# Weight parts in one buffer and one transfer, weight transfers issued by GpSimd, and 22 instead of 28 transfers in each pair's inverse, in a hybrid GLA and RWKV-7 layer

## The chip, the cores and the metric

The kernel runs on one core of a Trainium2 chip. The metric is the device time of one execution in microseconds (us), as the median of several runs. The core has five engines with an instruction queue each: TensorE (PE in the profile, with its weight loads as PEld), VectorE (DVE), ScalarE (ACT), GpSimd (POOL) and SyncE (SP), which computes nothing and here only issues transfers (DMA). Each queue works strictly in order: an instruction that waits for a semaphore holds up everything behind it on its engine. Sixteen DMA engines move the data between the core's memory (SBUF) and the chip's main memory (DRAM).

## The reference

One decoder layer on 1024 prompt tokens and 8 sample tokens. All of it in float32:

```python
p = einsum('btd,dn->btn', x, w_in)                 # 1024 -> 9360 columns
p_gla, p_rwkv, p_gate = split(p)
# GLA, 4 heads:  S_t = diag(a_t) S_{t-1} + k_t^T v_t ;  o_t = q_t S_t
# RWKV-7, 16 heads of 64:
#   S_t = S_{t-1} (diag(w_t) - kk_t^T (kk_t a_t)) + v_t^T k_t ;  y_t = S_t r_t
m = sigmoid(gate_a) * (o_gla @ w_up_gla) + sigmoid(gate_b) * (o_rwkv @ w_up_rwkv)
y = layernorm(alpha * x + m @ w_out)
```

The outputs are y for both groups of tokens, the new states of both branches and the last projected RWKV row.

## The kernel before, in words

**Matmuls in three parts.** TensorE's fast number format keeps fewer bits than float32, so every weight and every activation is split into a high part and a rest (low part), and each product is the sum of three matmuls: high by high, high by low, low by high. In the profile the weights' parts are `whi` and `wlo`, those of the activations `xh` and `xl`, and the three kinds of rows are `proj<-xh,whi`, `proj<-xl,whi`, `proj<-xh,wlo`.

**Two passes over the tokens.** The prompt is cut into two halves of 512 tokens; the first half carries the 8 sample tokens too. For each half the kernel goes through 73 blocks of 128 columns of `w_in`. After both, it multiplies with `w_up_gla` and `w_up_rwkv` (eight blocks each, for each half) and at last with `w_out`.

**The weights' way (`load_w`).** A block needs two pieces of 512 rows by 128 columns. In the first pass, a piece is loaded raw (`wraw<-w_in`, 256 KB, three buffers), cast to `whi` on ScalarE, subtracted to `wlo` on VectorE or GpSimd, and both parts are kept in DRAM (`wh<-whi`, `wl<-wlo`, 256 KB each). In the second pass the two parts are loaded back (`whi<-wh`, `wlo<-wl`) with no work for ScalarE and VectorE. `whi` and `wlo` have four buffers each. The 64 pieces of `w_up_gla` and `w_up_rwkv` are loaded raw and split each time.

**The RWKV pairs.** Heads are worked on in eight pairs for each half of the tokens, 16 in all, in chunks of 64 tokens. For each pair `front` makes a triangular matrix for each chunk and head (`GG`, tile `gg`), whose inverse is needed. The inverse goes by 32 by 32 blocks: the diagonal blocks are gathered through DRAM (`LD<-gg`, 4 transfers; `wide<-LD`, 4; the block below the diagonal `Lp<-gg`, 4), 31 steps of two VectorE instructions each invert all of them at once (`Xt<-X,wide` and `X<-X,Xt`), and the result goes back through DRAM (`XD<-X`, 4; `XT<-XD`, 4; `Xs<-XD`, 8). That is 28 transfers a pair. `back` and `turn` finish the inverse, `chain` runs the recurrence over the chunks on TensorE (`pch`), and `norm` writes `o_rwkv`.

**What sets the order.** The kernel is written as Python generators, one for each stream of work. A planner (class `Order`) asks each stream for its next operation, prices it (`price`, `transfer`), and writes down the operation that can start first by its own clock of each engine, with priorities (`PRIO`, `ON_PE`) between streams. The result is one fixed list of instructions for each engine. Where an operation may run on VectorE or on GpSimd (`self.E`), the planner takes the engine that it expects to end first. All transfers are issued by SP (`self.S`), in the planner's order. The transfers of one queue use eight semaphores in turn, so a transfer waits on its queue until the one eight places ahead of it has landed.

All instructions that the planner writes stand at one line of the code (L219 in the profile, the call inside a helper), so the groups in the profile are told apart by their tiles, not by their lines.

Of the kernel before, what the change touches and what calls it, by code (L numbers as in the profile page):

```python
# [20 lines left out]
P = 128  # L21
# [11 lines left out]
C = 64  # L33
# [20 lines left out]
WBUF = {"whi": ([P, 512], 4), "wlo": ([P, 512], 4), "wraw": ([P, 512], 3)}  # L54
# [8 lines left out]


# [82 lines left out]
def price(eng, name, out, args, ins):  # L147
# [60 lines left out]
class Engine:  # L208
# [3 lines left out]
    def __getattr__(self, name):  # L212
        def make(out, *args, **kw):
# [8 lines left out]
            if eng == "S":  # L222
# [18 lines left out]
class Order:  # L241
# [4 lines left out]
    def __init__(self, nc):  # L246
        self.P, self.A, self.V, self.G, self.S, self.E, self.C = (Engine(**e) for e in (
            {"P": nc.tensor}, {"A": nc.scalar}, {"V": nc.vector}, {"G": nc.gpsimd}, {"S": nc.sync},
# [82 lines left out]
    def start(self, op):  # L331

        best = None
        for eng, fn, cost in op.ways:
            free, t = self.time[eng] + (SWITCH if eng == "P" and op.tiles != self.tiles else 0.0), 0.0
            for x in (op.out, *op.ins):
                at, by = self.ready.get(x.tensor.name, (0.0, None))
                if eng == "S" and by == "D" and x is op.out:
                    continue
# [28 lines left out]
    def run(self):  # L368
        while self.streams:
# [24 lines left out]
            self.time[op.eng] = max(self.time[op.eng], t + cost)  # L394
# [8 lines left out]
            if op.eng == "S":  # L403
# [3 lines left out]
            self.ready[op.out.tensor.name] = end, "D" if op.eng == "S" else op.eng  # L407
# [5 lines left out]
class Kern(Order):  # L413
# [217 lines left out]
    def load_w(self):  # L631
# [5 lines left out]
        def keep(src, c0, j, hi, lo):  # L637
            for v, x in zip("hl", (hi, lo)):
                t = self.dr.tile([P, 512], F32, name=f"w{v}{c0}_{j}")
                kept.setdefault((c0, j), []).append(t)  # L640
                yield self.S.dma_start(t, x.bitcast(F32))

        def high():
            n = 0
            while True:
                yield lambda: len(raws) > n
                hi = yield from self.get("whi")
                yield self.A.copy(hi, raws[n][0])
                his.append(hi)
# [4 lines left out]
        def low():  # L654
            for n in range(count):
                yield lambda: len(his) > n
                lo = yield from self.get("wlo")
                raw, src, c0, j, i = raws[n]
                yield self.E.tensor_sub(lo, raw, his[n].bitcast(F32))
                self.free(raw)  # L660
                if src is self.a["w_in"] and i == 0:
                    yield from keep(src, c0, j, his[n], lo)
                self.ws.append((his[n], lo))
                los.append(lo)
# [18 lines left out]
    def blocks(self):  # L683
        xs = None
        for b in self.plan:
# [13 lines left out]
            while todo:  # L699
# [7 lines left out]
                for k in range(NK):  # L707
# [4 lines left out]
                    hi, lo = (x[:, k % 4 * P:k % 4 * P + P] for x in w[k // 4])  # L712
# [8 lines left out]
                    if fin and k % 4 == 3:  # L721
                        self.free(*w[k // 4])
# [378 lines left out]
    def front(self, c, p, st, d):  # L1101
# [4 lines left out]
        AZ, GG = (x.rearrange("p (c k h t) -> p c k h t", c=NCH, k=2, h=2) for x in (az, gg))  # L1106
# [83 lines left out]
        for q in range(4):  # L1190
            yield self.S.dma_start(L_[NU * q:NU * q + NU], LD.rearrange("n c s t -> (n c) (s t)"))
        Lp = (yield from self.get("Lp")).rearrange("p (y t) -> p y t", t=P)
        for n, b in enumerate(QS):
            h = n % 2
            yield self.S.dma_start(Lp[b, :, b], GG[QS[0], n // 2::2, 0, h, 32:64])
# [13 lines left out]
        for q in range(2):  # L1209
            b = slice(32 * q, 32 * q + 32)  # L1210
            for h in range(2):
                n = 2 * q + h
                yield self.S.dma_start(XT[HS[h]][b, :, h, b], XD[n * NCH:(n + 1) * NCH].rearrange("c s t -> s c t"))
        Xs = yield from self.get("Xs")
        xp = Xs[:, :2 * P].rearrange("p (q y t) -> p q y t", q=2, t=32)
        for n, b in enumerate(QS):
            for q in range(2):
# [579 lines left out]
```

## Time and profile before

| | us |
|---|---|
| median of 3 runs (lowest, highest) | 1544.31 (1543.3, 1545.22) |
| the profiled execution's own time | 1537.94 |
| span in the profile | 1536.1 |
| PE busy | 1492.0 |
| DVE busy | 1146.4 |
| ACT busy | 866.7 |
| POOL busy | 87.3 |
| moved by DMA | 330.68 MB in 377056 packets |

In the profile's views, "x146" counts instructions, and the idle time of an engine is put down to the instruction or transfer whose end released it. An entry such as `SPq` is time on SP's queue, which issues transfers. The first pass runs to about 600 us, the second to about 1211 us, the products with `w_up_gla` and `w_up_rwkv` to about 1430 us, and `w_out` fills the rest.

### The profile page before, as it was taken

To read this page: it belongs to the slowest core of one execution; us is meant where nothing else is said; L and a number is where in the kernel's file an instruction comes from. 1 tells how busy PE (TensorE), PEld (TensorE's weight loads), DVE (VectorE), ACT (ScalarE), POOL (GpSimd) and SP (SyncE) were. 2 spreads that over 40 slices of the span, in tenths; PEclk is the share of its full clock that TensorE was granted. 3 is DMA by queue.
4 is the path that set the end of the run, shared out by engine and by line. 5 is a ranking of instruction groups with operands and counts; after the bars stand their busy time and mean duration, and the time that the engine had idled before them with its cause. 6 is when DMAs were issued, how large, how long until landed. Compare 5 with 4: busy or idle time off the path is not lost. (4 is left out here: it accounts for less than half of the span.)

```text
span 1536.1 us, 32633 instructions
## 1 busy us (share of the span) xinstructions
PE 1492.0 (97%) x11352; PEld 1304.9 (85%) x11352; DVE 1146.4 (75%) x3044; ACT 866.7 (56%) x2218; POOL 87.3 (6%) x202
## 2 busy tenths in 40 slices
PE   9999989999999999999999999999999999999998
PEld 8999979899999998788777778878777898988786
DVE  5785879788968896777776888888875774665665
ACT  5665576667666676564654565456346745654210
POOL 0010000001000000000001020100100000000000
PEclk9999999999999999999999999999999999999999
DMA  9878968798869887865677557656664779798522
GB/s 302 268 224 245 323 191 256 200 294 255 256 172 291 251 264 201 254 179 147 170 210 197 166 151 215 203 156 185 181 206 117 239 212 270 243 289 276 182 87 83
DMA packets 377056, 330.68 MB, mean 215 GB/s; under 512 B 131219, under 2 KB 262428, under 8 KB 376892
## 3 DMA queue, kind: packets, MB, share of 16 engines
q1 hardware_dynamic: 376892, 328.60, 70.7%
q8 instruction: 90, 1.47, 0.4%
q14 instruction: 74, 0.61, 0.1%
HBM read 198.35 MB, written 118.61 MB: 206 GB/s over the span
## 5 line engine op out<-in xcount | busy, mean ns | idle before, releaser
L219 PE MATMUL proj<-xh,whi 128*128 128x264 f32 (+2 forms) x1880 | 618.3, 329 | 5.9 <-ACT whi L219 2.7
L219 PE MATMUL proj<-xh,wlo 128*128 128x264 f32 (+2 forms) x1880 | 617.7, 329 | 0.3 <-DVE wlo L219 0.2
L219 PE MATMUL proj<-xl,whi 128*128 128x264 f32 (+2 forms) x1880 | 617.7, 329 | 0.0
L219 PEld LDWEIGHTS proj<-xh,whi 128*128 128x128 f32 x1880 | 355.6, 189 | 32.6 <-ACT row L219 3.1
L219 PEld LDWEIGHTS proj<-xh,wlo 128*128 128x128 f32 x1880 | 356.0, 189 | 24.2 <-DVE wlo L219 1.0
L219 PEld LDWEIGHTS proj<-xl,whi 128*128 128x128 f32 x1880 | 356.0, 189 | 23.4 <-issue 1.4
L219 DVE TENSOR_TENSOR wlo<-wraw,whi 128x512 fp32r<-128x512 f32 x207 | 142.2, 690 | 73.6 <-ACT whi L219 65.0
L219 ACT CAST whi<-wraw 128x512 fp32r<-128x512 f32 x210 | 129.9, 620 | 98.6 <-PE proj L219 23.1
L219 DVE TENSOR_TENSOR row<-row 128x256 f32<-128x256 f32 (+8 forms) x330 | 165.2, 509 | 20.1 <-DMA row<-state_rwkv 6.7
L219 ACT ACTIVATE row<-row 128x512 f32<-128x512 f32 (+3 forms) x229 | 138.1, 610 | 19.2 <-DVE row L219 11.2
L219 DVE TENSOR_TENSOR Xt<-X,wide 128x60 f32<-128x60 f32 (+24 forms) x496 | 105.8, 213 | 26.4 <-DMA wide<-LD 14.1
L219 DVE TENSOR_TENSOR X<-X,Xt 128x60 f32<-128x60 f32 (+24 forms) x496 | 104.7, 211 | 12.2
L219 ACT COPY rh<-pch 128x128 f32<-128x128 f32 x116 | 30.9, 267 | 131.1 <-PE pch L219 130.6
L219 ACT ACTIVATE row<-proj,omu 128x256 f32<-128x256 f32 (+1 forms) x99 | 54.1, 548 | 69.6 <-PE proj L219 68.4
L219 PE MATMUL big<-row 128*128 128x128 f32 (+4 forms) x466 | 87.0, 323 | 5.9 <-DVE row L219 4.2
L219 ACT ACTIVATE s0p<-wide,pc 64x64 f32<-64x64 f32 x256 | 89.0, 347 | 1.9
L219 POOL TENSOR_TENSOR row<-row 128x256 f32<-128x256 f32 (+7 forms) x55 | 49.5, 904 | 573.4 <-DVE row L219 313.2
L219 DVE SCALAR_TENSOR_TENSOR wide<-pch,pc,s0p 64x64 f32<-64x64 f32 x224 | 63.0, 281 | 22.8 <-PE pch L219 18.8
L219 DVE SCALAR_TENSOR_TENSOR row<-proj,pv,row 128x255 f32<-128x255 f32 (+1 forms) x99 | 56.3, 569 | 24.7 <-ACT tail L219 14.8
L219 PEld LDWEIGHTS big<-row 128*128 128x128 f32 (+3 forms) x466 | 59.0, 179 | 17.5 <-ACT row L219 6.2
L219 ACT COPY row<-big 128x128 f32<-128x128 f32 (+5 forms) x146 | 42.8, 316 | 44.9 <-PE big L219 43.9
L392 ACT ACT_TABLE_LOAD x52 | 66.7, 1283 | 0.9
(282 smaller groups left out, 2472.9 us busy)
## 6 DMA issues: line engine op xcount, KB each, us to landing
wraw<-w_in SPq DMA_DIRECT2D x146, 256.0 KB
wh<-whi SPq DMA_DIRECT2D x146, 256.0 KB
wl<-wlo SPq DMA_DIRECT2D x146, 256.0 KB
whi<-wh SPq DMA_DIRECT2D x146, 256.0 KB
wlo<-wl SPq DMA_DIRECT2D x146, 256.0 KB
wide<-LD SPq DMA_DIRECT2D x64, 128.0 KB
wraw<-w_up_gla SPq DMA_DIRECT2D x32, 256.0 KB
wraw<-w_up_rwkv SPq DMA_DIRECT2D x32, 256.0 KB
```

What stands on the lines that cost most here:

```text
L219: ways.append((eng, lambda call=call: call(out, *args, **kw), price(eng, name, out, args, ins)))
L392: self.nc.scalar.preload_act_table_set(self.table)
```

## The change

Three things change, and the planner then writes a new order on all engines.

1. **One buffer for both parts.** `whi` and `wlo` become one tile `wb` of 1024 columns, high part in the first 512, low part in the last 512; four buffers as before, and the same bytes of SBUF. Keeping a piece in DRAM is one transfer of 512 KB where it was two of 256 KB, and so is loading it back.
2. **GpSimd issues the weights' transfers.** A new name `self.Q` stands for GpSimd as an issuer of transfers, with a price of 1.0 us in the planner (SP's is 0.48). All raw loads after the ninth, all 146 transfers that keep a piece and all 146 that load one back go there: 137 + 64 + 146 + 146 = 493. The first nine raw loads stay on SP. GpSimd has its own eight semaphores for transfers.
3. **22 transfers in an inverse.** The tile `GG` is laid out with the two halves of each chunk's columns outermost, so that `LD<-gg` takes 2 transfers where it took 4, and `Xs<-XD` 4 where it took 8. The bytes and the runs of 32 numbers stay as they were.

```diff
-WBUF = {"whi": ([P, 512], 4), "wlo": ([P, 512], 4), "wraw": ([P, 512], 3)}
+WBUF = {"wb": ([P, 1024], 4), "wraw": ([P, 512], 3)}
...
+SAME = {"Q": "G"}
...
+    if eng == "Q":
+        return 1.0
...
+            e = SAME.get(op.eng, op.eng)
+            self.time[e] = max(self.time[e], t + cost)
...
-        def keep(src, c0, j, hi, lo):
-            for v, x in zip("hl", (hi, lo)):
-                t = self.dr.tile([P, 512], F32, name=f"w{v}{c0}_{j}")
-                kept.setdefault((c0, j), []).append(t)
-                yield self.S.dma_start(t, x.bitcast(F32))
+        def keep(src, c0, j, x):
+            kept[c0, j] = self.dr.tile([P, 1024], F32, name=f"w{c0}_{j}")
+            yield self.Q.dma_start(kept[c0, j], x.bitcast(F32))
...
-                hi, lo = (yield from self.get("whi")), (yield from self.get("wlo"))
-                for x, t in zip((hi, lo), kept[c0, j]):
-                    yield self.S.dma_start(x.bitcast(F32), t)
-                self.ws.append((hi, lo))
+                x = yield from self.get("wb")
+                yield self.Q.dma_start(x.bitcast(F32), kept[c0, j])
+                self.ws.append(x)
...
-            op = self.S.dma_start(raw.rearrange("p (k c) -> p k c", c=P),
+            op = (self.Q if n > 8 else self.S).dma_start(raw.rearrange("p (k c) -> p k c", c=P),
...
-        LD = self.dr.tile([4, NCH, 32, 32], F32, name=f"LD{c.i}{p}")
+        LD = self.dr.tile([2, 2 * NCH, 32, 32], F32, name=f"LD{c.i}{p}")
         for q in range(2):
             b = slice(32 * q, 32 * q + 32)
-            for h in range(2):
-                yield self.S.dma_start(LD[2 * q + h].rearrange("c s t -> s c t"), GG[b, :, 0, h, b])
+            yield self.S.dma_start(LD[q].rearrange("u s t -> s u t"), GU[b, :, b])
...
         for n, b in enumerate(QS):
-            for q in range(2):
-                u = (2 * q + n % 2) * NCH + n // 2
-                yield self.S.dma_start(xp[b, q], XD[u:(2 * q + n % 2 + 1) * NCH:2].rearrange("c s t -> s c t"))
+            yield self.S.dma_start(xp[b], XD.rearrange("(m n) s t -> n s m t", n=4)[n])
```

Two places show what happens to the order. The first is the weight stream early in the first pass. Before, it stands on SP (`wh_…<-whi` and `wl_…<-wlo` keep the two parts of a piece, the numbers name the DRAM tile):

```order
L219 DMA wh_0_516<-whi 128x512
L219 DMA wraw<-w_in 128x4x128
L219 DMA wl_0_519<-wlo 128x512
L219 DMA row<-lora 64x512 x3
L219 DMA wh_1_567<-whi 128x512
L219 DMA wraw<-w_in 128x4x128
L219 DMA wl_1_574<-wlo 128x512
```

After the change, the same stream stands on GpSimd (POOL), one transfer to keep a piece for each raw load:

```order
L223 DMA wraw<-w_in 128x4x128
L223 DMA w_0_498<-wb 128x1024
L223 DMA wraw<-w_in 128x4x128
L223 DMA w_1_542<-wb 128x1024
L223 DMA wraw<-w_in 128x4x128
L223 DMA w_0_574<-wb 128x1024
```

Three SP entries for a piece have become two POOL entries, and nothing of the weights is left on SP between the other transfers.

The second place is the last pair's inverse, near the end of the RWKV work, with the loads of `o_rwkv` (`row<-o_rwkv`) for the next products right behind it. On SP before:

```order
L219 DMA XD_17660<-X 256x1x32 x4
L219 DMA row<-w_out 128x512 x2
L219 DMA wraw<-w_up_gla 128x4x128
L219 DMA mg_127<-row 128x520
L219 DMA XT_170<-XD_17660 32x8x32 x4
L219 DMA Xs<-XD_17660 32x4x32 x8
L219 DMA row<-o_rwkv 128x520
L219 DMA mg_128<-row 128x520
L219 DMA row<-o_rwkv 128x520 x7
L219 DMA az_168<-az_168 64x8x64
L219 DMA wraw<-w_up_gla 128x4x128
```

On SP after the change:

```order
L223 DMA XD_16836<-X 256x1x32 x4
L223 DMA row<-sg_97 128x520
L223 DMA row<-w_out 128x512
L223 DMA mg_127<-row 128x520
L223 DMA XT_170<-XD_16836 32x8x32 x4
L223 DMA Xs<-XD_16836 32x8x32 x4
L223 DMA az_168<-az_168 64x8x64
L223 DMA row<-sg_98 128x520
L223 DMA row<-o_rwkv 128x520
L223 DMA mg_128<-row 128x520
L223 DMA row<-o_rwkv 128x520 x7
```

`Xs<-XD` has four entries fewer, `az<-az` has moved ahead of the `o_rwkv` loads, and the `wraw` loads have left the queue. They stand on POOL, the 64 in a row:

```order
L223 MEMSET X 32x8 x4
L223 DMA wb<-w_0_9125 128x1024
L223 DMA wb<-w_1_9147 128x1024
L223 DMA wraw<-w_up_gla 128x4x128 x16
L223 DMA wraw<-w_up_rwkv 128x4x128 x16
L223 DMA wraw<-w_up_gla 128x4x128 x16
L223 DMA wraw<-w_up_rwkv 128x4x128 x16
```

On SP no weight load stands between the other transfers any more; on POOL nothing stands between these loads. TensorE's list has the same matmuls in a slightly different order. The planner, which now counts POOL's time for transfers, moves 22 additions and products of `row` tiles and 25 memsets of `X` from POOL to VectorE.

More of the change, by code (lines that the diff above doesn't have):

```diff
@@ L221, in make @@
                     port += eng
[L222 removed]
+            if eng in "SQ":
                 lag = transfer(out, args[0])
@@ L246, in __init__ @@
     def __init__(self, nc):
[L247 to L248 removed]
+        self.P, self.A, self.V, self.G, self.S, self.Q, self.E, self.C = (Engine(**e) for e in (
+            {"P": nc.tensor}, {"A": nc.scalar}, {"V": nc.vector}, {"G": nc.gpsimd}, {"S": nc.sync}, {"Q": nc.gpsimd},
             {"V": nc.vector, "G": nc.gpsimd}, {"A": nc.scalar, "V": nc.vector}))
@@ L334, in start @@
         for eng, fn, cost in op.ways:
-            free, t = self.time[eng] + (SWITCH if eng == "P" and op.tiles != self.tiles else 0.0), 0.0
+            free, t = self.time[SAME.get(eng, eng)] + (SWITCH if eng == "P" and op.tiles != self.tiles else 0.0), 0.0
             for x in (op.out, *op.ins):
                 at, by = self.ready.get(x.tensor.name, (0.0, None))
-                if eng == "S" and by == "D" and x is op.out:
+                if eng in "SQ" and by == "D" and x is op.out:
                     continue
@@ L406, in run @@
             end = max(end, self.ready.get(op.out.tensor.name, (0.0,))[0])
-            self.ready[op.out.tensor.name] = end, "D" if op.eng == "S" else op.eng
+            self.ready[op.out.tensor.name] = end, "D" if op.eng in "SQ" else op.eng
             for x in op.ins:
@@ L646, in high @@
                 yield lambda: len(raws) > n
-                hi = yield from self.get("whi")
-                yield self.A.copy(hi, raws[n][0])
-                his.append(hi)
+                x = yield from self.get("wb")
+                yield self.A.copy(x[:, :512], raws[n][0])
+                his.append(x)
                 n += 1
@@ L656, in low @@
                 yield lambda: len(his) > n
-                lo = yield from self.get("wlo")
+                x = his[n]
                 raw, src, c0, j, i = raws[n]
-                yield self.E.tensor_sub(lo, raw, his[n].bitcast(F32))
+                yield self.E.tensor_sub(x[:, 512:], raw, x[:, :512].bitcast(F32))
                 self.free(raw)
                 if src is self.a["w_in"] and i == 0:
-                    yield from keep(src, c0, j, his[n], lo)
-                self.ws.append((his[n], lo))
-                los.append(lo)
+                    yield from keep(src, c0, j, x)
+                self.ws.append(x)
+                los.append(x)
             self.w_done = True
@@ L711, in blocks @@
                         w.append(self.ws.pop(0))
-                    hi, lo = (x[:, k % 4 * P:k % 4 * P + P] for x in w[k // 4])
+                    hi, lo = (w[k // 4][:, x + k % 4 * P:x + k % 4 * P + P] for x in (0, 512))
                     xh, xl = xs[k]
@@ L721, in blocks @@
                     if fin and k % 4 == 3:
-                        self.free(*w[k // 4])
+                        self.free(w[k // 4])
                 for tt, t0, n, ps, q in qs:
@@ L1105, in front @@
         BK = BK_.rearrange("p (c t) -> p c t", c=NCH)
-        AZ, GG = (x.rearrange("p (c k h t) -> p c k h t", c=NCH, k=2, h=2) for x in (az, gg))
+        AZ = az.rearrange("p (c k h t) -> p c k h t", c=NCH, k=2, h=2)
+        GG = gg.rearrange("p (k c h t) -> p c k h t", c=NCH, k=2, h=2)
+        GU = gg[:, :2 * HT].rearrange("p (u t) -> p u t", t=C)
         if self.l2 is None:
@@ L1529, in split_out @@
             yield lambda: len(raws) > 2 * k
-            tag = "gg" if k < 2 else "wide" if k < 4 else None
+            tag = "gg" if k < 2 else "wide" if k < 4 else "wb" if k == 7 else None
             yield lambda: k < 7 or self.w_done
-            if tag == "wide":
+            if tag and k > 1:
                 parts = [[x[:, 0:512], x[:, 512:D]] for x in (yield from self.get(tag, 2))]
@@ L1539, in split_out @@
                 parts = [x[:2], x[2:]]
-            elif k < 7:
+            else:
                 parts = [[x[:, :512] for x in (yield from self.get("part", 2))], (yield from self.get("lw", 2))]
-            else:
-                parts = [(yield from self.get("whi", 2)), (yield from self.get("wlo", 2))]
             for hf in range(2):
```

15 lines of the change are left out of this document (7 added, 8 removed).

## The prediction

> **What bounds the kernel now.** I read the page's busy times first, then the busy time by stretches, then the waits of TensorE and of SP's queue, then the stretch where most idle time lies.
>
> ```profile
> PE 1492.0 (97%) x11352; PEld 1304.9 (85%) x11352; DVE 1146.4 (75%) x3044; ACT 866.7 (56%) x2218; POOL 87.3 (6%) x202
> ...
> q1 hardware_dynamic: 376892, 328.60, 70.7%
> ```
>
> TensorE is busy for 1492.0 of 1536.1 us, and the change leaves it the same 11352 matmuls. So at most 1536.1 - 1492.0 = 44.1 us are there to be won by anything that arrives earlier. Busy DMA time is 70.7%, so the transfers don't bound the whole. By stretches (PE, PEld, DVE, ACT, POOL busy, then clock, DMA share, GB/s):
>
> ```profile
> 0.00:50.00 50.00, 46.61 (x341) 42.30 (x342) 26.72 (x64) 27.98 (x60) 3.57 (x10) 1.00 0.92 296
> 200.00:300.00 100.00, 92.97 (x890) 86.77 (x891) 82.80 (x223) 69.37 (x191) 5.31 (x15) 0.97 0.72 214
> 700.00:800.00 100.00, 99.28 (x683) 81.24 (x682) 77.85 (x250) 56.03 (x147) 3.27 (x11) 1.00 0.57 163
> 800.00:900.00 100.00, 95.00 (x629) 75.65 (x628) 77.72 (x208) 54.21 (x142) 12.83 (x18) 0.98 0.65 182
> 1240.00:1300.00 60.00, 54.24 (x451) 52.94 (x450) 35.08 (x87) 29.47 (x57) 0.00 (x0) 0.97 0.82 241
> 1340.00:1536.00 196.00, 188.63 (x845) 152.11 (x844) 121.88 (x196) 61.58 (x126) 3.30 (x4) 0.99 0.56 182
> ```
>
> PE idles 3.4 us at the start, 7.0 in 200 to 300, 5.0 in 800 to 900, 5.8 around the step to the last products, and 7.4 in the last stretch. The start and the end hold 10.8 us that no transfer of weights can touch much; about 33 us lie between. What ends them:
>
> ```profile
> PEld big L219 <- ACT row L219: 13.5, 22, 4.7
> ...
> PE big L219 <- DVE part L219: 6.1, 4, 2.5
> PE big L219 <- DVE row L219: 5.1, 6, 2.0
> PE pch L219 <- DVE wide L219: 3.4, 4, 1.2
> PE proj L219 <- ACT whi L219: 2.7, 1, 2.7
> PE big L219 <- DMA S<-GS: 2.0, 1, 2.0
> PE pch L219 <- DMA wide<-Sd: 1.1, 1, 1.1
> PE pch L219 <- DMA az<-wide: 1.0, 2, 0.7
> ```
>
> The reader should see that most of it ends with VectorE and ScalarE, little with a transfer, and that PE waited for a weight's cast once. The weights are not late in the steady state.
>
> **The weights' transfers on GpSimd.** Here are the issues on SP, with shortest, median and longest duration in ns:
>
> ```profile
> L219 SPq DMA_DIRECT2D wh<-whi x146: 319/420/2216, 6.3 to 595.6; - x146
> L219 SPq DMA_DIRECT2D wl<-wlo x146: 319/556/1844, 10.0 to 596.5; - x146
> L219 SPq DMA_DIRECT2D whi<-wh x146: 319/341/943, 604.8 to 1210.8; - x146
> L219 SPq DMA_DIRECT2D wraw<-w_in x146: 378/396/1281, 1.2 to 589.6; - x146
> L219 SPq DMA_DIRECT2D wraw<-w_up_gla x32: 368/384/602, 1211.7 to 1369.2; - x32
> L219 SPq DMA_DIRECT2D wraw<-w_up_rwkv x32: 367/384/656, 1273.6 to 1413.6; - x32
> L219 POOL TENSOR_TENSOR wlo<-wraw,whi x3: 1286/1402/2272, 66.3 to 455.3; 128x512 fp32r<-128x512 f32 x3
> ```
>
> SP loses 584 issues for the kept parts and 201 raw loads. At about 0.4 us each that is 785 x 0.4 = 314 us of SP's time, but SP computes nothing; this is worth only what a transfer that PE awaits was held up by.
>
> The trace holds no transfer issued by POOL. From below an issue costs SP's 0.4 us; from above I take twice POOL's own work on a whole 128x512 tile, 2 x 1.40 = 2.8 us, because a raw load is 512 runs where that work is 128 rows. I take 1.4, POOL's row itself, since the engine is the same. POOL's budget follows from the pace of the stream. In the first pass, 145 steps from 1.2 to 589.6 us give 4.06 us for a piece, in which POOL must issue a raw load and a keep: 2.8 us at my price, and with POOL's other work, 87.3 / 1536 x 4.06 = 0.23 us, 3.0 of 4.06. In the second pass it is one load in (1210.8 - 604.8) / 145 = 4.18 us. In the last products it is one raw load in (1413.6 - 1211.7) / 63 = 3.20 us. All three fit. The term is 0, and POOL becomes the bound where a raw load and a keep together pass 4.06 - 0.23 = 3.8 us.
>
> A later landing is covered too. Three raw buffers at 4.06 us each make a round of 12.2 us. A round spends one landing (the longest on the chain of waits is below, 5.95 us), a cast of 0.62 us and a subtraction of 0.69 us. That leaves some 4.9 us for a slower issue. In the last products the round is 9.6 us and 2.3 us are left, then the four `wb` buffers, two blocks ahead of PE. If that cover went, each piece would cost PE what its round is too long, divided by three.
>
> By the Trainium skill, page SBUF — State Buffer, section "SBUF: two separate sides", a transfer issued by GpSimd stalls while VectorE copies float32 within SBUF, since GpSimd cannot then write the descriptors. These are the rows of such copies:
>
> ```profile
> L219 DVE CAST part<-row 128x512 fp32r<-128x512 f32 (+1 forms) x42 | 17.9, 427 | 12.7 <-ACT row L219 10.3 <-PE big L219 1.8
> L219 DVE COPY row<-row 128x128 f32<-128x128 f32 (+2 forms) x25 | 5.3, 226 | 0.0
> L219 DVE COPY pc<-row 128x8 f32<-128x8 f32 (+1 forms) x32 | 5.3, 164 | 0.2
> ```
>
> They last 28.5 us in all. By that rule, and with every one of them in front of an issue that PE awaits, the sum would be 28.5 us worse; spread over the run it is 2% of POOL's time. I give it no term, because the two to five us of cover are longer than any one of these copies.
>
> **What SP's queue gains.** The one weight that PE awaited was late because of SP's order. SP in that stretch, then the chain of waits there:
>
> ```profile
> 1253.34 2.53 SPq L219 DMA_DIRECT2D XD<-X  x4
> ...
> 1258.65 1.99 SPq L219 DMA_DIRECT2D XT<-XD  x4
> 1260.69 4.88 SPq L219 DMA_DIRECT2D Xs<-XD  x8
> 1265.62 0.43 SPq L219 DMA_DIRECT2D row<-o_rwkv  x1
> 1266.14 0.38 SPq L219 DMA_DIRECT2D mg<-row  x1
> 1266.57 4.04 SPq L219 DMA_DIRECT2D row<-o_rwkv  x7
> 1270.65 0.64 SPq L219 DMA_DIRECT2D az<-az  x1
> 1271.38 0.60 SPq L219 DMA_DIRECT2D wraw<-w_up_gla  x1
> ```
>
> ```profile
> 1267.57 5.34 DMA row<-o_rwkv
> 1272.97 5.95 DMA wraw<-w_up_gla
> ```
>
> ```profile
> 1277.45 0.62 ACT L219 CAST whi<-wraw 128x512 fp32r<-128x512 f32 x1 [13.01 <-DMA wraw<-w_up_gla]
> ```
>
> From 1258.65 to 1271.3 SP issues one transfer after another, and the raw load of `w_up_gla` stands behind all of them; ScalarE then waits 13.01 us for it, and PE 2.7 us for ScalarE. On POOL the load has nothing in front of it but its own free buffer. I count the 2.7 us as won. `Xs<-XD` with four issues fewer saves 4.88 / 2 = 2.4 us of SP here, and `az<-az`, now ahead of eight `o_rwkv` entries, goes some 5 us earlier; but PE works on other products meanwhile, so this is worth nothing further unless the pair ends late. If that work ran out, it would be up to the other 3.1 us of idle time here.
>
> Elsewhere, transfers ended 2.0 + 1.1 + 1.0 = 4.1 us of PE's idle time (`S<-GS`, `wide<-Sd`, `az<-wide`). With no weights in front of them, and a queue and semaphores of their own, I take half, 2 us; the ends are 0 and 4.1. At the start, the raw loads to the ninth no longer share SP with the keeping of parts: I take 1 us of the 3.4 that PE idles up to 50 us, between 0 and 3.4.
>
> By the Trainium skill, page DMA: Bandwidth & Descriptors, section "Issuing engines are not separate DMA queues", issuing from several engines saves only the time to issue, usually small beside the transfer. By that rule the 2 us for shorter waits would fall to almost nothing, while the 2.7 us, which are a matter of issue order, would stay.
>
> **The rest.** VectorE takes over 22 `row` operations and 25 memsets:
>
> ```profile
> L219 DVE TENSOR_TENSOR row<-row 128x256 f32<-128x256 f32 (+8 forms) x330 | 165.2, 509 | 20.1 <-DMA row<-state_rwkv 6.7
> L219 POOL MEMSET X<- 32x8 f32 (+1 forms) x80 | 12.2, 152 | 82.5 <-DMA XD<-X 79.0
> ```
>
> That is 22 x 0.51 + 25 x 0.15 = 15 us of VectorE. VectorE's three large rows in PE's waits hold 6.1 + 5.1 + 3.4 = 14.6 us for 1146 us of its work, 1.3%, so I charge 15 x 1.3% = 0.2 us; all of it on the path would be 15. The new layout of `GG` changes no matmul and no run of 32 numbers: 0.
>
> Sum: -2.7 - 2 - 1 + 0.2 = -5.5 us. On the profiled execution, 1537.94 - 5.5 = 1532.4; on the median, which lies 6.4 us above that execution, 1544.3 - 5.5 = 1538.8. A new order also redraws the other 25 us of idle time, which ended with VectorE and ScalarE, by some us either way. With fewer transfers in the way of 16 inverses I expect that draw to fall to the better side by 1.6 us, half of the 3.1 us that the step to the last products still holds idle, and say 1537.
>
> **The rivals.**
>
> *Hidden anyway.* PE's idle time stays, since VectorE and ScalarE end most of it; the 2.7 us come back as another wait. For it: the rows of PE's waits. Against it: the 13.01 us. Time: 1542 to 1547.
>
> *POOL becomes the bound.* If an issue costs 2 us and more, the first pass runs at POOL's pace. At 2.1 us each a piece takes 2 x 2.1 + 0.23 = 4.43 us, 0.37 over its 4.06, and 146 pieces lose 54 us, less the 5.5: about 1593. At the point from which it decides, 1.9 us, it loses nothing; halfway, at 2.0, it is 0.17 x 146 = 25 us, about 1564. For it: 512 runs in a raw load, and POOL's longest subtraction took 2.27 us. Against it: POOL is 94% idle now.
>
> *The new order meets VectorE.* The 15 us more of VectorE work fall where PE waits for VectorE, as in 800 to 900 us. All of it on the path less the 5.5: 1544.3 + 9.5 = 1554.
>
> *More is won.* All idle time between start and end goes, 33 us: 1511. Half of it: 1528.
>
> **How the numbers follow.** A measurement of this kernel tells about 0.2%, 3 us, from no change. I give 0.42 to the forecast, 0.13 to more (1528 and below), 0.18 to hidden, 0.15 to the new order meeting VectorE, 0.12 to POOL as the bound. Faster is the forecast and more: 0.55. Same takes 0.18, slower 0.27. The forecast's own range is 1531 to 1541. The wide one reaches from 1518, between the two figures for more, to 1562, beyond the case of VectorE and just short of POOL at 2.0 us.
>
> **What would show it.** If the steps are right, POOL's issues of weights take under 1.9 us each on average; ScalarE's 13 us wait for `wraw<-w_up_gla` is gone; PE's idle time between 50 and 1340 us falls from about 33 to about 27 us; SP's issue rows number about 870. If casts wait for `wraw<-w_in` for far more than now and PE waits for `wb`, POOL is the bound. If SP's waits shrink and PE's idle time stays, the gain was hidden. If PE's new waits end with DVE `row`, it was the order.

## The result, and the profile after

The changed kernel takes 1554.99 us (median of 4 runs, 1551.57 to 1556.65) against 1544.03 us of the kernel before in the same comparison (4 runs, 1543.3 to 1545.22). The ratio is 1.0073, 95% interval [1.0052, 1.0095]: slower by 11 us, where 7 us less was predicted. The profiled execution has a span of 1552.9 us, 16.8 us longer than before. One execution among all that are reported here, of the kernel with the 22 transfers alone, took 2915.9 us; it is in that kernel's median below, and the ratio leaves it out.

The page of the changed kernel: busy times, then the DMA queues (packets, MB, share of 16 engines).

```profile
PE 1499.3 (97%) x11352; PEld 1305.9 (84%) x11352; DVE 1155.9 (74%) x3102; ACT 868.6 (56%) x2216; POOL 372.6 (24%) x641
...
q0 software_dynamic: 58128, 205.81, 41.8%
q1 hardware_dynamic: 185132, 122.76, 28.0%
```

The weights' 205.81 MB now have a queue of their own. The two queues together are as busy (69.8%) as the one was (70.7%). PE is idle for 1552.9 - 1499.3 = 53.6 us where it was 44.1, and busy for 7.3 us more with the same matmuls: its mean granted clock fell from 0.995 to 0.990.

GpSimd's issues and SP's nine raw loads, duration in ns as shortest, median and longest:

```profile
L223 POOL DMA_DIRECT2D w<-wb x146: 534/545/763, 7.0 to 607.5; - x146
L223 POOL DMA_DIRECT2D wb<-w x146: 531/531/748, 619.5 to 1237.8; - x146
L223 POOL DMA_DIRECT2D wraw<-w_in x137: 757/757/832, 29.2 to 587.2; - x137
L223 POOL DMA_DIRECT2D wraw<-w_up_gla x32: 749/749/771, 1238.3 to 1386.3; - x32
L223 SPq DMA_DIRECT2D wraw<-w_in x9: 368/391/927, 1.2 to 26.8; - x9
```

An issue costs GpSimd 0.53 to 0.76 us (a raw load twice SP's 0.39), and a raw load with its keep 1.3 us of the 4.06 us of a piece. GpSimd is not the bound.

PE's idle time by stretches (the columns are those of the prediction's rows):

```profile
0.00:50.00 50.00, 45.19 (x329) 41.02 (x330) 25.87 (x63) 25.84 (x57) 15.46 (x28) 0.97 0.87 280
200.00:300.00 100.00, 90.19 (x834) 81.79 (x833) 86.22 (x232) 66.68 (x173) 32.97 (x55) 0.95 0.68 208
600.00:700.00 100.00, 94.52 (x704) 75.39 (x703) 71.84 (x186) 61.32 (x158) 17.04 (x35) 0.95 0.70 208
700.00:800.00 100.00, 91.84 (x591) 74.59 (x590) 72.87 (x233) 53.08 (x139) 15.85 (x26) 0.98 0.60 166
800.00:900.00 100.00, 97.98 (x697) 78.39 (x697) 85.80 (x248) 55.83 (x147) 16.51 (x33) 1.00 0.66 186
1240.00:1300.00 60.00, 58.81 (x516) 55.91 (x515) 41.80 (x120) 33.75 (x66) 13.28 (x18) 1.00 0.87 257
```

The step to the last products idles 1.2 us where it idled 5.8, as predicted. The second pass loses more than that: PE idles 8.2 us against 0.7 in 700 to 800, and 5.5 against 1.2 in 600 to 700. Over the whole second pass, of the kernel before and then of the changed one:

```profile
600.00:1240.00 640.00, 624.43 (x4298) 506.56 (x4298) 492.17 (x1377) 359.43 (x919) 46.53 (x91) 1.00 0.64 186
```

```profile
600.00:1240.00 640.00, 612.86 (x4185) 492.94 (x4184) 489.30 (x1380) 355.75 (x909) 118.99 (x220) 0.99 0.64 182
```

PE idles 27.1 us there and idled 15.6. What PE's waits in the changed kernel end with (total, times, longest):

```profile
PE big L223 <- DVE part L223: 6.3, 9, 1.2
PE pch L223 <- DVE wide L223: 5.0, 8, 1.4
PE big L223 <- DVE Xs L223: 3.8, 1, 3.8
PE big L223 <- DMA S<-GS: 3.6, 2, 3.1
PE big L223 <- DVE row L223: 3.5, 4, 2.0
PE big L223 <- ACT part L223: 2.8, 1, 2.8
```

No weight is among these longest ones, and GpSimd neither. `S<-GS` (a state of the GLA branch, read back) and, by way of VectorE's transpose, `Xs` come from transfers on SP, the queue that the change was to set free.

### The profile page after: what moved, and what is told of

It reads as the page before. It is cut to its first block, busy times and chain, and to the rows that moved or that the text cites. A ratio compares the mean times of both kernels' runs of the same rounds, so it can differ in the third digit from the quotient of the medians.

```text
span 1552.9 us, 32046 instructions
## 1 busy us (share of the span) xinstructions
PE 1499.3 (97%) x11352; PEld 1305.9 (84%) x11352; DVE 1155.9 (74%) x3102; ACT 868.6 (56%) x2216; POOL 372.6 (24%) x641
## 3 DMA queue, kind: packets, MB, share of 16 engines
q0 software_dynamic: 58128, 205.81, 41.8%
## 4 chain that ended last, share of the span: by engine, by line
PE 70%; DVE 15%; DMA 5%; ACT 4%; issue 3%; SPq 1%; POOL 0%; POOLq 0%; DVEq 0%; ACTq 0%
PE proj L223 42%; PE big L223 16%; PE pY L223 8%; DVE row L223 6%; PE pch L223 4%; DVE Xt L223 2%; DVE X L223 2%; ACT row L223 2%; DVE wide L223 1%; DMA wide<-LD 1%; DVE wb L223 1%; SPq L223 1%; DMA wraw<-w_in 1%; DVE part L223 1%; DMA row<-xT 1%
## 5 line engine op out<-in xcount | busy, mean ns | idle before, releaser
L223 PE MATMUL proj<-xh,wb 128*128 128x256 f32 (+2 forms) x3760 | 921.0, 328 | 2.5 <-DVE row L223 1.9
L223 PEld LDWEIGHTS proj<-xh,wb 128*128 128x128 f32 x3760 | 630.3, 189 | 51.8 <-issue 5.4
L223 PE MATMUL proj<-xl,wb 128*128 128x264 f32 (+2 forms) x1880 | 614.4, 327 | 0.0
L223 PEld LDWEIGHTS proj<-xl,wb 128*128 128x128 f32 x1880 | 355.8, 189 | 22.6 <-issue 1.2
L223 DVE TENSOR_TENSOR wb<-wraw,wb 128x512 fp32r<-128x512 f32 x208 | 142.8, 687 | 83.9 <-ACT wb L223 82.3
L223 POOL DMA_DIRECT2D wb<-w x146 | 79.2, 543 | 492.0 <-PE proj L223 396.8
L223 POOL DMA_DIRECT2D wraw<-w_in x137 | 104.3, 761 | 337.9 <-DVE wb L223 199.9
L223 ACT CAST wb<-wraw 128x512 fp32r<-128x512 f32 x210 | 130.2, 621 | 84.2 <-PE proj L223 27.1
L223 POOL DMA_DIRECT2D w<-wb x146 | 79.9, 547 | 38.3 <-DVE wb L223 24.8
L223 PE MATMUL big<-xh,wb 128*128 128x512 f32 (+2 forms) x272 | 69.9, 331 | 0.0
```

The costliest lines, as they stand in the source:

```text
L223: ways.append((eng, lambda call=call: call(out, *args, **kw), price(eng, name, out, args, ins)))
```

## The experiments

Three theories stood at the start. **A**: a second queue makes SP's own transfers land later. **B**: the planner drew a worse order. **C**: the larger transfers or the common buffer cost. Ratios are against the kernel before, with their 95% intervals; "same order" means that the lists of PE, VectorE and ScalarE agree operation by operation. No experiment leaves out any computation of the layer.

### Which part of the change costs

The 22 transfers alone, added to the kernel before (a short part of the diff; all the rest of part 3 with it):

```
-            for h in range(2):
-                yield self.S.dma_start(LD[2 * q + h].rearrange("c s t -> s c t"), GG[b, :, 0, h, b])
+            yield self.S.dma_start(LD[q].rearrange("u s t -> s u t"), GU[b, :, b])
```

> The kernel before with the 22 transfers an inverse alone: two weight buffers, all transfers on SP, planned anew. Theory A: 1538 to 1545 us. Theory B: anywhere within 8 us of the kernel before, since any edit draws a new order. Theory C in the form that the inverse's longer transfers cost: 1550 or more.

Measured: 1533.26 us, ratio 0.9944 [0.9922, 0.9966]. **Faster**: the part that the prediction gave nothing, together with the order that the planner drew for it, is a gain of 8.6 us.

The changed kernel with the weights back on SP, the planner left to draw its order for that:

```
-{"S": nc.sync}, {"Q": nc.gpsimd},
+{"S": nc.sync}, {"S": nc.sync},
```

> One buffer and 22 transfers an inverse, but the weights' transfers stay on SP and the planner knows it, so it writes an order of its own. Theory A (second queue): 1538 to 1545 us. Theory B (the order drawn with GpSimd's price): also 1538 to 1547, an order drawn anew. Theory C (the larger transfers): 1552 to 1558.

Measured: 1557.46 us, 1.0105 [1.0082, 1.0129].

The changed kernel's own order, with only the queue that issues the weights changed:

```
-{"Q": nc.gpsimd},
+{"Q": nc.sync},
```

> The change in full, with the planner's order as it stands after the change on every engine, but the weights' transfers are issued by SP instead of GpSimd: only the queue differs. Theory A (the second queue is the cost: the traces show SP's own transfers landing later after the change, for example Lp<-gg in 6.2 us where it took 3.1, since weights no longer stand in line with them): back to about 1540 to 1546 us. Theory B (the new order of work is the cost, whoever issues): stays at 1552 to 1558. Theory C (transfers of 512 KB or the longer ones in the inverse are the cost): stays at 1552 to 1558 too. SP may also be late with an order that was planned without its issue time: then above 1558.

Measured: 1546.73 us, 1.0024 [1.0005, 1.0042].

The order planned for SP, with the weights issued by GpSimd:

```
-{"S": nc.sync}, {"S": nc.sync},
+{"S": nc.sync}, {"S": nc.gpsimd},
```

> The same order on TensorE, VectorE and ScalarE as in the run planned for SP, instruction for instruction, but the weights' transfers after the ninth raw load are issued by GpSimd. Theory A: 8 to 12 us slower than the run planned for SP. Theory B and C: within 3 us of it.

Measured: 1581.91 us, 1.0259 [1.0234, 1.0285], 24 us more than with the weights on SP, twice what theory A expected. So with the order held, GpSimd's queue costs 1.0073 - 1.0024 = 0.5% in the changed kernel's order and 1.0259 - 1.0105 = 1.5% in the other. Between the 22 transfers alone and the kernel planned for SP, both on SP, lie 1.6% that can be B or C.

### Order held: queue and buffer apart

Three runs stay in the order of the 22 transfers alone, and four only draw an order anew. First GpSimd as the issuer of all weights but the first nine raw loads, still two buffers and 256 KB. `Q` is priced by the planner as SP and issued by GpSimd:

```
+            {"P": nc.tensor}, {"A": nc.scalar}, {"V": nc.vector}, {"G": nc.gpsimd}, {"S": nc.sync}, {"S": nc.gpsimd},
...
-                yield self.S.dma_start(t, x.bitcast(F32))
+                yield self.Q.dma_start(t, x.bitcast(F32))
...
-                    yield self.S.dma_start(x.bitcast(F32), t)
+                    yield self.Q.dma_start(x.bitcast(F32), t)
...
-            op = self.S.dma_start(raw.rearrange("p (k c) -> p k c", c=P),
+            op = (self.Q if n > 8 else self.S).dma_start(raw.rearrange("p (k c) -> p k c", c=P),
```

> The 22 transfers a pair alone ran at 0.9944 of the kernel before. This kernel keeps that one's order on TensorE, VectorE and ScalarE operation by operation, and its two buffers and transfers of 128x512; only the weights' transfers behind the ninth raw load are issued by GpSimd. Theory A (a second queue makes SP's own transfers land later): slower than with SP by the 0.5% to 1.5% that the two pairs of equal order showed, so 0.999 to 1.009, with wide<-LD and Xs<-XD landing later than on SP. Theory B (the order alone made the change slower): no difference, 0.992 to 0.997. Theory C (a 512 KB transfer is what lands late and holds others up): these are still 256 KB, so little of A's loss, 0.994 to 0.998.

Measured: 1556.72 us, 1.0085 [1.0052, 1.0118]. Then one buffer and one transfer of 512 KB, on SP; the planner is shown the two halves as two tiles, so it draws the same order, and of its two transfers only the second one is written down, with all 1024 columns:

```
+            x = wp.tile([P, 1024], F32R, name="wb", bufs=4)
+            self.seconds.append(x[:, 512:])
+            return x[:, :512]
...
+            op.ways = [(eng, lambda: nc_dma(out, x.bitcast(F32)) if second else None, cost)]
```

> Again the order of the 22 transfers alone, operation by operation on TensorE, VectorE and ScalarE, all on SP; but a weight's two parts lie in one buffer of 128x1024 and are kept and loaded by one transfer, which SP issues where the second one stood. Theory C (the larger transfer or the common buffer costs): what lies between the 22 transfers alone (0.9944) and the version planned with one buffer on SP (1.0105), so 1.005 to 1.012. Theory B (that difference of 1.6% was the order that the planner drew, not the buffer): 0.991 to 0.997, like the 22 alone. Theory A says nothing of it.

Measured: 1538.51 us, 0.9965 [0.9948, 0.9983]. Both together, which is the whole change in that order (the raw loads behind the ninth on GpSimd too):

```
-        nc_dma = self.nc.sync.dma_start
+        nc_dma = self.nc.gpsimd.dma_start
```

> The whole change, one buffer, one transfer of 512 KB, 22 transfers a pair and GpSimd's queue, but in the order of the kernel with the 22 transfers alone (operation by operation on TensorE, VectorE and ScalarE). Theory A (queue): 0.999 to 1.009. Theory A and C together (queue and size): 1.010 to 1.022. Theory B (only the planner's new order lost): 0.992 to 0.997, and then the change would have been a gain in a good order.

Measured: 1565.43 us, 1.0144 [1.0108, 1.0180]. The queue costs 1.4% with two buffers and 1.8% with one; the buffer 0.2% on SP, where the intervals overlap. Theory A holds, and theory C falls for SP. On GpSimd's queue the one buffer adds 0.6% (1.0144 against 1.0085), and the intervals only just touch (1.0108 and 1.0118); 1.0144 lies where A and C together were expected, so a part of C stays open there. And the kernel before with one constant of the planner moved:

```
-HOP = {"P": 0.2, "D": 0.8, "G": 0.14, "V": 0.14, "A": 0.14}
+HOP = {"P": 0.2, "D": 0.82, "G": 0.14, "V": 0.14, "A": 0.14}
```

> The kernel before with one of its planner's constants moved by a little (the delay that it assumes behind a transfer, 0.80 to 0.82 us). Nothing that is computed, issued or stored changes, but the planner draws another order. Theory B (an order drawn anew is worth as much as the whole change): it differs from 1 by 0.4% to 1.2%, either way. Theories A and C need orders to be worth little: 0.998 to 1.002.

Measured: 1581.42 us, 1.0247 [1.0219, 1.0275]. The same work in another order is worth more than three times the whole change. So theory B, too, can make a loss of this size. The same edit, `"D": 0.8` to `"D": 0.82`, in the kernel with the 22 transfers alone:

> The kernel with the 22 transfers alone, with the planner's delay behind a transfer moved from 0.80 to 0.82 us: the same work in another drawn order. The redrawn kernel before was 2.5% off. Theory B (orders differ by a per cent or more whatever the edit): it lies off 0.9944 by 0.5% or more, likely above 1.000. If the 22 transfers are worth 0.56% in any order and the redrawn kernel before was a freak: 0.992 to 0.998.

Measured: 1532.32 us, 0.9934 [0.9912, 0.9956].

The same edit in the changed kernel:

> The changed kernel with the same constant moved from 0.80 to 0.82 us. Theory B: it lies off 1.0073 by 0.5% or more, either way. If orders are worth little and the queue and the buffer make the loss: 1.005 to 1.010.

Measured: 1541.17 us, 1.0001 [0.9981, 1.0020].

A third draw of the kernel before, with `"D": 0.78`:

> The kernel before with the planner's delay behind a transfer at 0.78 in place of 0.80 us: a third draw of its order (0.82 gave 1.0247). If orders commonly differ by a per cent: off 1 by 0.4% or more, either way. If the draw at 0.82 was a freak: 0.997 to 1.003.

Measured: 1560.23 us, 1.0130 [1.0104, 1.0156]. So the kernel before ran in the best of three orders (1, 1.013, 1.025), and the changed kernel as measured in the worse of two (1.007, 1.000). Both draws with the 22 transfers alone (0.994, 0.993) lie below all draws of the kernel before. But no run has 28 and 22 transfers in one and the same order, so how much of the 0.6% belongs to the transfers and how much to the order is not separated. A shorter inverse in the second pass is not shown either: as measured further below, an inverse of the last eight pairs took 45.6 us before, 46.6 with the 22 transfers and 44.3 with these redrawn.

### Which transfers make the queue's loss

In the order of the 22 transfers alone again, two buffers, with only some of the weights issued by GpSimd. Raw loads alone:

```
-            op = self.S.dma_start(raw.rearrange("p (k c) -> p k c", c=P),
+            op = (self.Q if n > 8 else self.S).dma_start(raw.rearrange("p (k c) -> p k c", c=P),
```

> The order of the 22 transfers alone (0.9944) on TensorE, VectorE and ScalarE; of the weights only the raw loads behind the ninth (201 transfers of 256 KB, in runs of 512 bytes) are issued by GpSimd, the kept parts stay on SP. All weights on GpSimd in this order gave 1.0085, 1.4% more. If each issue or each byte on the second queue costs alike, the raw loads, a quarter of the bytes and of the issues, bring a quarter of it: 0.997 to 0.999. If the raw loads, whose issue takes GpSimd longest (0.76 us), or the waits of GpSimd for a free raw buffer are what hurts, most of it: 1.003 to 1.008. If it is the kept parts with their large packets, nothing: 0.993 to 0.996.

Measured: 1532.56 us, 0.9938 [0.9918, 0.9959]: nothing lost. Kept parts alone, stored and loaded:

```
-                yield self.S.dma_start(t, x.bitcast(F32))
+                yield self.Q.dma_start(t, x.bitcast(F32))
...
-                    yield self.S.dma_start(x.bitcast(F32), t)
+                    yield self.Q.dma_start(x.bitcast(F32), t)
```

> The counterpart: the raw loads stay on SP, the kept parts (584 transfers of 256 KB, in rows of 2 KB) are issued by GpSimd, in the same order of the other engines. Alike per issue or byte: three quarters of the 1.4%, 1.003 to 1.007. If the kept parts are the cause alone: 1.007 to 1.010. If the raw loads are: 0.993 to 0.997.

Measured: 1555.12 us, 1.0093 [1.0066, 1.0121]: all of it. The stores alone (the first of these two edits):

> All kept parts on GpSimd cost 1.5% (1.0093 against 0.9944), the raw loads nothing (0.9938). Here only the stores of the first pass (292 transfers of 256 KB from SBUF to DRAM) are issued by GpSimd; order of TensorE, VectorE and ScalarE as before. By the stretches of TensorE's busy time, the kept parts on GpSimd lost 4 us of PE each in 600 to 800 and in 800 to 1000 us, where the second pass loads them, and nothing in 400 to 600. If it is the loads: 0.992 to 0.998. If it is the rows of 2 KB whichever way they go: about half, 1.001 to 1.004. If it is the stores: 1.006 to 1.010.

Measured: 1542.50 us, 1.0010 [0.9997, 1.0023], above what was expected if the loads alone are the cause.

The loads alone (the second one):

> Only the second pass's loads of kept parts (292 transfers of 256 KB from DRAM) are issued by GpSimd; else as the 22 transfers alone. If it is the loads: 1.005 to 1.010, with PE's busy time lower in 600 to 1000 us by some 8 us. If it is the rows of 2 KB whichever way: 1.001 to 1.004. If it is the stores: 0.992 to 0.998.

Measured: 1560.07 us, 1.0112 [1.0098, 1.0125]. The loads cost 1.7%, no less than stores and loads together (the intervals overlap). The stores alone cost 0.7%, and in the pair of both they cost nothing, so the two don't add; why the stores cost alone stays open. In the changed kernel itself, with only the loads back on SP (`on_sp` leaves the planner's price as it is and writes the transfer to SP's queue):

```
-                yield self.Q.dma_start(x.bitcast(F32), kept[c0, j])
+                yield on_sp(self.Q.dma_start(x.bitcast(F32), kept[c0, j]), x, kept[c0, j])
```

> The changed kernel in its own order; only the 146 loads of kept parts (512 KB each) go back from GpSimd to SP. The changed kernel ran at 1.0073, with all its weights on SP at 1.0024. If the loads make the queue's loss: 1.000 to 1.004. If the stores: 1.006 to 1.010. If in this order the queue's loss is spread: 1.004 to 1.006.

Measured: 1545.27 us, 1.0022 [1.0012, 1.0033], the same as with all weights on SP. So the loads of the second pass make the queue's whole loss in the changed kernel as well, as far as these intervals tell, and its second pass shows it; this kernel's row, to be held against the changed kernel's above:

```profile
600.00:1240.00 640.00, 619.73 (x4218) 499.32 (x4219) 491.43 (x1384) 360.64 (x923) 40.84 (x75) 0.99 0.64 184
```

PE gets 6.9 us back there.

### What the loads do to SP's transfers

One pair's inverse, the sixth of the second pass, on SP's queue. The 22 transfers alone (start, duration, issue):

```profile
1064.47 0.98 SPq L219 DMA_DIRECT2D LD<-gg  x2
1065.55 0.45 SPq L219 DMA_DIRECT2D whi<-wh  x1
1066.09 0.39 SPq L219 DMA_DIRECT2D wlo<-wl  x1
1066.58 0.38 SPq L219 DMA_DIRECT2D o_gla<-row  x1
1067.11 1.72 SPq L219 DMA_DIRECT2D wide<-LD  x4
...
1092.32 2.54 SPq L219 DMA_DIRECT2D XD<-X  x4
```

With the loads on GpSimd, SP's queue, its wait there, and GpSimd's queue:

```profile
1082.86 0.98 SPq L219 DMA_DIRECT2D LD<-gg  x2
1083.93 0.46 SPq L219 DMA_DIRECT2D o_gla<-row  x1
1088.58 1.77 SPq L219 DMA_DIRECT2D wide<-LD  x4
...
1111.88 2.53 SPq L219 DMA_DIRECT2D XD<-X  x4
```

```profile
SPq L219 <- DMA LD<-gg: 4.0, 1, 4.0
```

```profile
1083.24 0.58 POOL L219 DMA_DIRECT2D whi<-wh  x1
1083.82 0.54 POOL L219 DMA_DIRECT2D wlo<-wl  x1
```

On SP two weights are issued *behind* `LD<-gg`, and the read-back `wide<-LD` starts 2.6 us after it. With the loads on GpSimd, two weights are issued in the same microsecond on the other queue, beside it; SP has less to issue, and stands 4.0 us for `LD<-gg` to land, so the read-back starts 5.7 us after it. VectorE's waits for that read-back, without and with the loads on GpSimd, over the whole run:

```profile
DVE Xt L219 <- DMA wide<-LD: 12.8, 5, 9.3
```

```profile
DVE Xt L219 <- DMA wide<-LD: 25.5, 6, 10.7
```

For all pairs I took from the traces' DMA events the time from the start of the issue to the last completion of each transfer. Medians of those issued from 600 to 1240 us: `LD<-gg` 2.09 us with the loads on SP and 3.14 on GpSimd, `wide<-LD` 3.90 and 5.04, `Lp<-gg` 3.21 and 5.36, `XD<-X` 1.94 and 2.74, `Xs<-XD` 1.89 and 3.11; only `XT<-XD` fell, from 2.92 to 2.58. In the changed kernel's order, with all weights on SP and then on GpSimd, `wide<-LD` goes from 4.90 to 5.77, `Lp<-gg` from 4.09 to 5.98, `XD<-X` from 2.02 to 3.13 and `Xs<-XD` from 2.84 to 3.34, while `LD<-gg` falls from 3.60 to 2.37. In the same way, the time of an inverse from its first `LD<-gg` issue to its last `Xs<-XD` landed, as a mean of the last eight pairs, and the time from the ninth pair's start to the sixteenth's:

| order | kernel | loads by | inverse, us | ninth to sixteenth, us | ratio |
|---|---|---|---|---|---|
| 22 alone | 22 transfers alone | SP | 46.6 | 532.6 | 0.9944 |
| | one buffer | SP | 46.7 | 532.4 | 0.9965 |
| | raw loads on GpSimd | SP | 46.6 | 533.1 | 0.9938 |
| | stores on GpSimd | SP | 46.5 | 531.7 | 1.0010 |
| | kept parts on GpSimd | GpSimd | 49.5 | 546.4 | 1.0093 |
| | all weights on GpSimd | GpSimd | 49.5 | 548.6 | 1.0085 |
| | loads on GpSimd | GpSimd | 49.7 | 552.1 | 1.0112 |
| | one buffer, all on GpSimd | GpSimd | 49.9 | 554.6 | 1.0144 |
| of the changed kernel | all weights on SP | SP | 50.3 | 531.9 | 1.0024 |
| | its loads on SP | SP | 50.1 | 535.8 | 1.0022 |
| | the changed kernel | GpSimd | 50.5 | 539.9 | 1.0073 |

In the first order the split is clean. Loads on GpSimd make an inverse 3 us longer, and the seven steps from the ninth pair to the sixteenth 14 to 22 us longer, 2 to 3 us each. That is most of the 22 to 28 us that these runs lose: the second pass runs at the pace of the pairs. In the changed kernel's order the inverse hardly grows (0.2 to 0.4 us) and the steps grow by 4 to 8 us, of the 8 us that the queue costs there. One place where they arise can be seen: SP's `S<-GS`, which reads back a state of the GLA branch. First with all weights on SP, then SP, GpSimd and PE in the changed kernel:

```profile
734.68 0.60 SPq L223 DMA_DIRECT2D S<-GS  x1
735.38 0.38 SPq L223 DMA_DIRECT2D wb<-w  x1
```

```profile
736.18 0.60 SPq L223 DMA_DIRECT2D S<-GS  x1
...
736.04 0.53 POOL L223 DMA_DIRECT2D wb<-w  x1 [2.57 <-PE big L223]
...
742.41 0.73 PE L223 MATMUL big<-row,S 128*128 128x128 f32 x2 [3.10 <-DMA S<-GS]
```

With a weight's load issued behind it, `S<-GS` lands 2.32 us after the start of its issue; with one beside it, after 6.18 us, and PE stands 3.1 us for it. Matmul by matmul, PE in the changed kernel is 1.5 us later than with the weights on SP ahead of this place, and 4.8 us later at it. What else carries the 8 us was not separated. The raw loads lengthen the first pass's transfers in the same way (`wide<-LD` from 4.14 to 5.74 us up to 600 us, with the raw loads alone on GpSimd), but that pass doesn't get longer by it.

Two other ways in which the loads could do it were looked at. GpSimd stands for a free buffer ahead of each load, with its own work behind it. With the loads on SP, and a memset that makes GpSimd stand at the same places:

```
+                self.nc.gpsimd.memset(x[:32, :8], 0.0)
                 self.nc.sync.dma_start(x, t)
```

> The 22 transfers alone with all its transfers on SP, but ahead of each of the 292 loads of kept parts GpSimd clears 32x8 numbers of the buffer, so that it stands in its own queue for the buffer to come free where it stood to issue the load, and its own work (80 memsets of X and others) stands behind it; the load itself is SP's. If GpSimd's own work, held up behind the loads, makes the loss of 1.7% that loads on GpSimd brought (1.0112 against 0.9944): 1.005 to 1.013. If it is a second queue's transfers beside SP's: 0.994 to 0.999 (a little is lost since the load waits for the memset).

Measured: 1536.24 us, 0.9963 [0.9945, 0.9982]; an inverse takes 46.4 us. So standing explains some 0.2% of the 1.7%. In the changed kernel VectorE did once wait for a product of GpSimd's that stood behind a load, and with all weights on SP it did not:

```profile
DVE Xt L223 <- POOL row L223: 4.0, 1, 4.0
```

PE lost nothing by it: matmul by matmul, it is 10.3 us later than with the weights on SP before this wait and 9.5 us after it.

The other: GpSimd's packets are larger. With the loads alone on GpSimd, the trace records their data there as 18688 packets of 4096 bytes, 159 ns each in the median; the same loads on SP are packets of 2048 bytes, 84 ns. With loads on GpSimd, and the kept parts stored and loaded as 512 runs of 512 bytes, as the raw loads are:

```
-                t = self.dr.tile([P, 512], F32, name=f"w{v}{c0}_{j}")
+                t = self.dr.tile([4 * P, P], F32, name=f"w{v}{c0}_{j}")
```

> Loads on GpSimd once more, but the kept parts lie in DRAM so that stores and loads go in runs of 512 bytes (as the raw loads, which cost nothing on GpSimd) in place of 2 KB. If large packets beside SP's small ones make the loss: 0.995 to 1.004. If it is GpSimd's standing, or a second queue whatever its packets: 1.009 to 1.016.

Measured: 1564.34 us, 1.0140 [1.0112, 1.0168]; an inverse takes 49.7 us, as with 2 KB. But on GpSimd's queue the trace still records 18688 packets of 4096 bytes, now 173 ns each: this run changed the layout of the kept parts and the packets of SP's stores, not the packets that run beside SP's transfers. So it does not tell whether smaller packets would cost less. (Runs of 512 bytes with the loads on SP were not measured, so what they cost by themselves is not known either.)

That a load beside a transfer makes it late shows within one run. With the loads on GpSimd, `Xs<-XD` in the second pass lands after 1.91 us where no weight's load is under way at the end of its issue (5 transfers, medians), and after 3.21 us where one is (27); `XD<-X` after 1.94 us (7) and 3.09 (25). In the changed kernel it is 1.86 (9) and 3.81 us (23), and 1.92 (3) and 3.21 (29). With the loads on SP, only 9 of the 32 `Xs<-XD` and 10 of the 32 `XD<-X` meet one. Without a load beside them they are thus as fast as on SP, whose medians were 1.89 and 1.94 us. Whether loads on another engine's queue, or in smaller packets, would cost as much, no run here tells. By the Trainium skill, page DMA: Bandwidth & Descriptors, section "Queues, rings and completion order", each DMA engine serves the queues that have work for it in turn, a packet at a time. The runs agree with it in direction (`LD<-gg` lands after 3.14 us in place of 2.09); the turns themselves no run shows.

## Why the prediction was wrong, point by point

**What bounds the kernel.** Right: PE, with its idle time as the prize. The prediction took the second pass's waits for VectorE as VectorE's own. In part they are the end of a chain that runs through SP's transfers (VectorE's `Xt` waited 14.1 us for `wide<-LD`, and 18.0 us in the changed kernel), and it is this chain that the change made longer. The first row that it gives for what ends PE's idle time, 13.5 us behind `ACT row`, is one of PEld, which idles 1536.1 - 1304.9 = 231.2 us in all; PE's own row is smaller:

```profile
PE big L219 <- ACT row L219: 5.6, 4, 4.2
```

And it took PE's busy time as fixed: of the 16.8 us that the profiled execution grew, 9.5 are idle time, and 7.3 are the same matmuls at a lower granted clock.

**GpSimd's price.** Taken as 1.4 us, measured 0.53 to 0.76, nearer the lower end (0.4). The conclusion, no bound by GpSimd, was right. By the Trainium skill, page SBUF — State Buffer, section "SBUF: two separate sides", issues should have stalled under VectorE's copies; the longest of GpSimd's issues in the rows above took 0.83 us, so the issue rows show no such stall.

**-2.7 us for the load of `w_up_gla`.** The place was right: ScalarE's wait of 13 us is gone. Now:

```profile
ACT wb L223 <- DMA wraw<-w_up_gla: 6.3, 6, 2.4
```

PE's idle time in 1240 to 1300 us fell by 4.6 us. But GpSimd isn't needed for it: with all weights on SP, the 22 transfers alone show this wait at 2.6 us in all, and the changed kernel's order at 3.2. It was a matter of the order alone.

**-2 us for shorter waits, "with no weights in front of them, and a queue and semaphores of their own".** This is the step that failed. It counted only what stands in front of a transfer on its queue, and not what then runs beside it; so it had the sign wrong, and waits grew where they were to shrink (`S<-GS` from 2.0 to 3.6 us of PE's idle time). Measured, the loads' queue costs 0.5% (8 us) in the changed kernel's order and 1.7% (26 us) in another. It is not the whole miss: with all weights back on SP the changed kernel stands at 1.0024, where the prediction had 0.995, and the rest lies with the order (below). By the Trainium skill, page DMA: Bandwidth & Descriptors, section "Issuing engines are not separate DMA queues", the step was worth almost nothing; that was nearer, but these runs show a loss.

**-1 us at the start.** Wrong: PE idles 4.8 us up to 50 us, and idled 3.4. All weights on SP in the same order leave it at 3.6 (46.43 us busy of 50), so by these two executions that loss, too, is mostly the queue's.

**0 for the 22 transfers.** Mis-sized: with the orders drawn for them they are the change's one gain, 0.6% in both draws, though the transfers' own share of it is not separated. The prediction looked at SP's 2.4 us in one place, where PE had other work, and not at 16 pairs.

**0 for one buffer.** About right on SP: 0.2% with the order held, within the intervals. On GpSimd's queue it is 0.6%, barely within them.

**+0.2 us for VectorE, and -1.6 us for the draw.** VectorE's busy time rose by 9.5 us, not 15 (the trace has 26 `row<-row` instructions less on GpSimd, and 25 memsets). The draw was named, with "some us either way", and then given a hopeful sign; three draws of the kernel before span 2.5%, 38 us. The changed kernel, with all weights on SP in its own order (1.0024), lies 0.8% above the 22 transfers alone; the buffer explains 0.2% of it, and the other 0.6% is left for the order, by subtraction; no run shows it by itself.

**The rivals.** Hidden anyway: no, what was to be hidden came true and was outweighed. GpSimd as the bound: no. The new order meeting VectorE gave the right time (1554) by luck: its mechanism is VectorE's added work, and with the same work in the same order, but the weights on SP, the kernel takes 1546.73 us. The rival that was missing is theory A.

**The signs.** Three of the four came true: GpSimd's issues took well under 1.9 us, the 13 us wait was gone, and SP issued 871 transfers. None of them looked at when SP's transfers land. The fourth failed: PE's idle time between 50 and 1340 us rose from 33.3 to 41.1 us, in place of falling to 27.

So the change is, in ratios, and as far as parts from different orders may be added: -0.6% for the 22 transfers with their order, +0.5% for the loads on GpSimd, some +0.2% for the one buffer, and +0.6% for the order, together +0.7%. The best that the runs found are the 22 transfers without the rest: 0.9934 redrawn, 0.9938 with the raw loads on GpSimd, 0.9944 as they stand, which these intervals don't tell apart.

## What to carry to other kernels

A transfer that is taken off a queue doesn't leave the machine: on a queue of its own it runs beside what it used to stand behind, so first ask whether short transfers in a chain of dependent ones run at the same time. Merging small transfers of a chain went with the one gain here. Where a planner draws the whole order, change one constant that means nothing and measure how far the time moves, and hold the order fixed to see what an edit itself is worth.

## What was not expected of the hardware

A second queue made the first one's small transfers land later: `Lp<-gg`, 16 KB each, from 3.21 to 5.36 us in the second pass, at the same total of DMA work (54.3 + 16.1 = 70.4% busy against 71.1%). GpSimd's queue carried the loads in packets of 4096 bytes, with rows of 2 KB and with runs of 512 bytes alike, where SP's had 2048. GpSimd issues a transfer in 0.53 us where it has 128 rows, and in 0.76 us where it has 512 runs of 512 bytes. PE's idle time alone does not tell the granted clock: 0.998 at 40.3 us idle (the 22 transfers alone), but 0.990 at 41.1 (one buffer on SP); 0.990 at 53.6 (the changed kernel), but 0.996 at 58.3 (kept parts on GpSimd); and 0.980 at 73.4 (the kernel before redrawn at 0.82).
